# The recurrence of a two-layer decoder: the carried products' first half moved ahead of the values' products, and the sample's states summed over 80 rows

## The chip, the cores and the metric

The kernel runs on one core of one Trainium2 chip. The metric is the device time of one execution in microseconds (us), as the median of several executions. A core has engines that run side by side, each with its own instruction order: PE (matrix products, with PEld, the loading of its weights), DVE (vector), ACT (activations), POOL (GpSimd) and SP, which here mostly issues DMAs. PE works on 128 x 128 elements; a product can use all of it, 64 rows of it, or 64 columns of it, and two products that use different halves can run side by side. Results land in PSUM banks, and another engine has to copy them out before a bank is used again.

## The reference

One inference step of a decoder with two layers, a prompt of 1024 tokens behind 16 meta tokens, and a sample of 8 sequences with 8 tokens each. The first layer is an mLSTM, the second a forgetting attention; each is followed by a SwiGLU. The change lies in the mLSTM, whose recurrence goes over chunks of tokens. In a chunk, for each of 8 heads (`m_t` is a running maximum, `b` the summed log forget gates):

```python
s = jnp.einsum('bhtk,bhsk->bhts', q, k) * jnp.exp(dmat - m_t[..., None])
num = w_inter[..., None] * jnp.einsum('bhtk,bhkv->bhtv', q, C) + jnp.einsum('bhts,bhsv->bhtv', s, v)
den = w_inter * jnp.einsum('bhtk,bhk->bht', q, n) + jnp.sum(s, axis=-1)
h = num / jnp.maximum(jnp.abs(den), jnp.exp(-m_t))[..., None]
C_new = w_c[..., None, None] * C + jnp.einsum('bhs,bhsk,bhsv->bhkv', w_g, k, v)
```

In words: the scores `s` weigh the values of the chunk, the state `C` carried from earlier chunks is read with the queries, and the new state adds the chunk's keys and values. `n` runs along as a 129th column of `C`. The output `h` is normalised per head, multiplied with the sigmoid of an output gate and projected. The sample's tokens do the same, one chunk for each sequence, each with a state of its own.

## The kernel before

Everything is f32; a large product is split into three (high by high, high by low, low by high parts; `mm3`, lines 193 to 195). The tokens lie in nine tiles: tile 0 has 80 rows, 64 of the sample and 16 meta tokens, and tiles 1 to 8 have 128 prompt tokens each. A tile is a chunk of the recurrence.

`recurrence` (line 1155) writes the order of PE, DVE, ACT and POOL by hand: an instruction stands on its engine where the Python code issues it (`manual_schedule`). What it interleaves with the chunks is called fill: `f(1)` issues one step, three matmuls, of the output gates' product. Eight steps fill a PSUM bank (tag `mmA`, two banks); ACT then takes the sigmoid into `stg` (line 960) and POOL stores it to `ogD` (line 961). There are 192 such steps, and they run out within chunk 7. From then on `g` issues gate heads instead (`gate_head`, line 1549): three transposes on PE, the product with the gate on DVE (line 1559), a rounded copy on ACT (line 271) and the rest on DVE (line 272).

Iteration i of the loop does this for chunk i and the next ones, the code that issues it in brackets:

- scores of chunk i+1 (`chunk_scores`): eight 64-row products into two `sps` banks (line 1352), multiplied into `eb` on DVE (line 1354); two steps of fill; then its keys: four transposes into a bank `kps` of the same tag (line 1358), `kw` on DVE (line 1360), and the weighted queries `wb` (line 1362);
- the state (`chunk_state`): two banks `cp` of 64-column products (line 1391), added to `C` on DVE (line 1395), and on POOL `Cw`, the decayed state for the next chunk (line 1398);
- the decay of chunk i+2 (`decay_steps`): eight operations of DVE on `eb` (line 1335), whose exponential ACT takes later (line 1338);
- the output of chunk i (`chunk_out`): twice, for z = 0 and 1, values' products over the whole array (line 1453) and carried products of 64 rows (line 1457) into the two banks tagged `nps`; DVE copies the denominators (`den`, line 1415) and ACT the values (`vA`, line 1423), which frees the banks; at the end the exponential and the squares (line 1472);
- in iterations 3 and 6 the norm of the three chunks before (`norm_heads`, lines 1524 to 1542): five small DVE operations, a square root on ACT, two more and three long ones on DVE. The root needs another table in ACT than the sigmoid, and the exponential a third.

`chunk_load` (line 1268) has POOL issue the loads of `qk`, `eb` and `wb` of chunk i+2 at the head of iteration i, in POOL's queue with the stores to `ogD`.

Ahead of the loop, chunk 0 also updates the sample's eight states (`first_states`, line 1483): for four pairs of sequences and eight heads a product `cs` (line 1498) of the keys `km` (64 rows, masked by `bm` to one pair, line 1479) with the values, and on DVE the update of `C0` (line 1499), with a step of fill behind every second product. Behind the recurrence the output product (`pops`) starts, with weights `wo` that SP loads (line 512).

Of the kernel before, what the change touches and what calls it, by code (L numbers as in the profile page):

```python
# [8 lines left out]
F32 = mybir.dt.float32  # L9
# [8 lines left out]
P = 128  # L18
# [1015 lines left out]
def rec_prep(self, kp, gates, rp, pp):  # L1034
# [3 lines left out]
    if True:  # L1038
# [15 lines left out]
        for j in range(4):  # L1054
            for a in range(2):
# [14 lines left out]
                                channel_multiplier=1)  # L1070
        nc.gpsimd.affine_select(out=cap0[:, NS:], in_=cap0[:, NS:], compare_op=ALU.is_ge, fill=NEG, base=-NS,
                                pattern=[[0, NM]], channel_multiplier=1)
        bm = kp.tile([NS, NB], F32, name="bm")
        nc.gpsimd.memset(bm, 1.0)
        nc.gpsimd.affine_select(out=bm, in_=bm, compare_op=ALU.is_ge, fill=0.0, base=0, pattern=[[-8, 8]],
                                channel_multiplier=1)
# [77 lines left out]
@_add(Net)  # L1154
def recurrence(self, kp, rec, v, qkD, fill, gate):


    nc, I, O = self.nc, self.I, self.O
    eD, wD, cap, cap0, wcP, wcS, bm = rec
    tm, den, ssq = self.fin  # L1160

    self.fills = 0

    def f(n):
        for _ in range(n):
            next(fill, None)
            self.fills += 1

    C = self.C
    E = mybir.EngineType  # L1170
    with ExitStack() as cr, self.pool("recAp", bufs=2, space=PSUM) as pp:
        order = ExitStack()
        order.enter_context(self.tc.manual_schedule(engines={E.PE, E.DVE, E.Activation, E.Pool}))
        args = (pp, kp, C, v, qkD, eD, wD, tm)

        r0 = cr.enter_context(self.pool("rec0"))
        sets = {1: r0}
        load = lambda i: self.chunk_load(i, sets[i % 3], *args)
        with self.pool("sampA") as sp:
            R = self.chunk_load(0, r0, *args)  # L1180
            N = dict(eb=r0.tile([P, HA, P], F32, name="eb1", tag="eb", bufs=2))
            self.first_load(R, sp)
            f(4)
            self.chunk_decay(0, R, tm, cap0)
            R["exp"]()
            f(6)
            self.chunk_scores(0, R, r0, *args, f)
            self.first_queries(R, sp)
            f(2)
            self.first_sums(R, pp)  # L1190
            self.first_keys(0, R, bm)
            f(3)
            self.chunk_state(0, R, *args, wcP, f)
            N = self.chunk_load(1, r0, *args, **N)
            self.chunk_out(0, R, r0, *args, den, ssq, f, sp)

            ahead = r0.tile([P, HA, P], F32, name="eb2", tag="eb", bufs=2)
            nc.gpsimd.dma_start(ahead, eD[:, TT[2][0] : TT[2][1]].partition_broadcast(P))
            self.first_states(R, sp, pp, v, wcS, bm, f, self.decay_steps(1, N, tm, cap), N)
        with self.pool("rec2") as sets[2], self.pool("rec1", bufs=2) as rp, self.pool("rec3") as sets[0]:  # L1200
            R, N = N, self.chunk_load(2, sets[2], *args, eb=ahead, loaded=True)
            self.chunk_decay(2, N, tm, cap)
            N["exp"]()
            f(10)
            self.chunk_scores(1, R, rp, *args, f)
            g, norm = f, iter(())
            places = []
            gate = gate(places)
            for i in range(1, NT):
                N2 = load(i + 2) if i + 2 < NT else None  # L1210
                if i + 1 < NT:
                    f(12 if i == 1 else 3)
                    self.chunk_scores(i + 1, N, rp, *args, f)
                next(norm, None)
                g(2)
                self.chunk_state(i, R, *args, wcP, g)
                if i == NT - 1:
                    state = self.last_state(C[i % 2], pp, rp)
                    next(state)
                if N2:  # L1220
                    self.chunk_decay(i + 2, N2, tm, cap)
                next(norm, None)
                self.chunk_out(i, R, rp, *args, den, ssq, g, exp=N2 and N2["exp"],
                               then=(lambda: next(state, None)) if i == NT - 1 else None)
                for _ in norm:
# [64 lines left out]
@_add(Net)  # L1290
def first_load(self, R, sp):

    nc, I = self.nc, self.I

    W = 4 * 96 + 16
    qq = sp.tile([P, 512 + 2 * W], F32, name="qq")
    R["q2"] = qq[:, :512].rearrange("p (j z t) -> p j z t", z=2, t=NS)
    R["qms"] = [qq[:, 512 + z * W : 512 + z * W + W] for z in range(2)]
    R["y"] = [sp.tile([P, 2, DV], F32, name=f"y{g}") for g in range(4)]

    R["km"] = [sp.tile([NS, HA, 2, DK], F32, name="km0"),
               qq[:NS, : HA * P].rearrange("p (h a k) -> p h a k", h=HA, a=2)]
# [39 lines left out]
def chunk_scores(self, i, R, rp, pp, kp, C, v, qkD, eD, wD, tm, f):  # L1342
# [9 lines left out]
            nc.tensor.matmul(sps[g][:L, j, :L], qk[r, 4 + j, :L], qk[r, j, :L], start=True, stop=True)  # L1352
    for g in range(2):
        nc.vector.tensor_tensor(out=eb[:L, g::2, :L], in0=sps[g][:L, :, :L], in1=eb[:L, g::2, :L], op=ALU.mult)
    f(2 if i else 6)
    kps = pp.tile([P, 4, P], F32, name=f"kps{i}", tag="sps")
    for j in range(4):
        nc.tensor.transpose(kps[:L, j, :], qk[:, 4 + j, :L], self.ident)
# [41 lines left out]


@_add(Net)
def chunk_out(self, i, R, rp, pp, kp, C, v, qkD, eD, wD, tm, den, ssq, f, sp=None, exp=None, then=None):

    nc = self.nc
    L = TT[i][1] - TT[i][0]
# [16 lines left out]
            nc.scalar.copy(v(i)[:L, hx, :DV], ps[:L, :, :DV])  # L1423

    new = lambda g: pp.tile([P, 2, DV + 1], F32, name=f"nps{i}{g}", tag="nps")
    if i == 0:
        for g, hs in enumerate(((0, 2), (4, 6), (1, 3), (5, 7))):
            f(4)
# [13 lines left out]
            done(ps, g, hs)  # L1442
    else:

        for z in range(2):
            f(2 if z == 0 else 3)
            if z:
                f(3)
            ps = [new(2 * z + a) for a in range(2)]
            for a in range(2):  # L1450
                for x in range(2):
                    h = 4 * z + 2 * x + a
                    nc.tensor.matmul(ps[a][:L, x, :], at[:L, h, :L], v(i)[:L, h, :], start=(x == 0), stop=False)
            for x in range(2):
                for a in range(2):
                    r = slice(a * 64, a * 64 + 64)
                    nc.tensor.matmul(ps[a][:L, x, :], qw[r, 2 * z + x, :], Cp[r, 2 * z + x, :], start=False, stop=(x == 1))
            for a in range(2):
                done(ps[a], 2 * z + a, (4 * z + a, 4 * z + 2 + a))
        f(1)  # L1460
    if exp:
        exp()
    if then:
# [11 lines left out]
@_add(Net)  # L1475
def first_keys(self, j, R, bm):

    for a in range(2):
        self.nc.vector.tensor_scalar_mul(R["km"][j % 2][:, :, a, :], R["kw"][:NS], bm[:, 2 * j + a : 2 * j + a + 1])


@_add(Net)
def first_states(self, R, sp, pp, v, wcS, bm, f, steps, N):
# [3 lines left out]
    for j in range(4):  # L1487
        if j == 3:
            for _ in steps:
                pass  # L1490
            N["exp"]()
        else:
            self.first_keys(j + 1, R, bm)
        km = R["km"][j % 2]
        f(2)
        for h in range(HA):
            ps = pp.tile([P, DV + 1], F32, name=f"cs{j}{h}", tag="cps")
            nc.tensor.matmul(ps, km[:, h, :, :].rearrange("p a k -> p (a k)"), v(0)[:NS, h, :], start=True, stop=True)
            nc.vector.scalar_tensor_tensor(out=C0[:, j, h, :], in0=C0[:, j, h, :], scalar=wcS[:, j, h : h + 1],
                                           in1=ps, op0=ALU.mult, op1=ALU.add)  # L1500
            if h % 2:
                f(1)
                if j:
                    next(steps, None)
# [1541 lines left out]
```

## Time and profile before

| | us |
|---|---|
| runs of the kernel before | 2814.28, 2818.92, 2822.15 |
| their median | 2818.92 |
| the profiled execution, first to last instruction (span) | 2818.5 |
| PE busy, in the profiled execution | 2762.3 |
| DVE busy | 1798.8 |
| ACT busy | 1177.1 |
| POOL busy | 856.1 |

The profiled execution's time is its span and what lies around it; only the span is listed. It stands at the median of the runs. Times in rows of the profile are microseconds from the span's start. A row gives start, duration, engine, line, operation, output <- inputs, the tile of PE, the shape and a count of records; in square brackets stands the time for which the engine sat idle ahead of it and the instruction that ended the idle time. The recurrence takes the stretch from about 230 to 417 us. PE's clock was 0.994 of the full one in the mean of the span.

### The profile page before, as it was taken

The numbers are of one execution on the slowest core, as the hardware profiler recorded it, in microseconds if no ns is written. First come the engines' busy times: TensorE is split into PE (matmuls) and PEld (weight loads), VectorE is DVE, ScalarE is ACT, GpSimd is POOL, SyncE is SP. The second block draws the span as 40 slices with busy tenths as digits, with TensorE's granted clock in tenths as the row PEclk, the third lists the DMA queues.
The fourth block names the chain that finished last, engine by engine and source line by source line (L and its number), as shares of the span: only waits on it lengthen the run. The fifth ranks groups of instructions, "written<-read, shape, count | busy, mean of one in ns | idle before, by whom it ended". The sixth has DMA issues, their size and how long they took to land. (4 is left out here: it accounts for less than half of the span.)

```text
span 2818.5 us, 60631 instructions
## 1 busy us (share of the span) xinstructions
PE 2762.3 (98%) x23543; PEld 2650.7 (94%) x23543; DVE 1798.8 (64%) x4025; ACT 1177.1 (42%) x2299; POOL 856.1 (30%) x1348
## 2 busy tenths in 40 slices
PE   9999989999999999999999999999999999999998
PEld 8998879999999999999999887677999999999998
DVE  5633566888887655662455444776388888766656
ACT  5432553422223334443444455777343223323345
POOL 3142333223223232124452202444313223323111
PEclk9999999999999999999999999999999999999999
DMA  7666555355564375544443775432524655527556
GB/s 213 174 188 170 151 164 193 108 152 158 173 178 137 120 246 171 192 145 163 145 173 123 264 293 193 161 128 87 157 87 126 177 176 163 162 91 236 179 195 215
DMA packets 432420, 474.05 MB, mean 168 GB/s; under 512 B 37015, under 2 KB 358291, under 8 KB 431107
## 3 DMA queue, kind: packets, MB, share of 16 engines
q1 hardware_dynamic: 380562, 320.52, 36.9%
q0 software_dynamic: 44928, 143.44, 15.5%
q10 hardware_dynamic: 6640, 6.21, 0.7%
q8 instruction: 185, 3.03, 0.5%
q14 instruction: 105, 0.85, 0.1%
HBM read 322.84 MB, written 147.21 MB: 167 GB/s over the span
## 5 line engine op out<-in xcount | busy, mean ns | idle before, releaser
L1614 PE MATMUL m<-xh,slot 128*128 128x276 f32 x2752 | 541.0, 290 | 1.8 <-ACT fs L1643 1.8
L1614 PEld LDWEIGHTS m<-xh,slot 128*128 128x128 f32 x2752 | 440.1, 188 | 3.6 <-ACT fs L1643 2.2
L1614 PE MATMUL m<-xl,slot 128*128 128x276 f32 x1376 | 397.3, 289 | 0.0
L1614 PEld LDWEIGHTS m<-xl,slot 128*128 128x128 f32 x1376 | 259.0, 188 | 0.0
L193 PE MATMUL tmps<-slot,xh 128*128 128x256 f32 (+2 forms) x864 | 243.1, 281 | 0.0
L195 PE MATMUL tmps<-slot,xl 128*128 128x256 f32 (+2 forms) x864 | 240.6, 278 | 0.0
L194 PE MATMUL tmps<-slot,xh 128*128 128x256 f32 (+2 forms) x864 | 240.5, 278 | 0.0
L272 DVE TENSOR_TENSOR slot<-slot,slot 128x1024 fp32r<-128x1024 f32 x124 | 162.9, 1314 | 60.1 <-ACT slot L271 58.7
L271 ACT CAST slot<-slot 128x1024 fp32r<-128x1024 f32 x124 | 129.5, 1045 | 142.6 <-PE m L1614 111.7
L194 PEld LDWEIGHTS tmps<-slot,xh 128*128 128x128 f32 (+1 forms) x864 | 159.1, 184 | 0.1
L195 PEld LDWEIGHTS tmps<-slot,xl 128*128 128x128 f32 (+1 forms) x864 | 158.6, 184 | 0.0
L193 PEld LDWEIGHTS tmps<-slot,xh 128*128 128x128 f32 (+1 forms) x864 | 158.4, 183 | 0.2
L193 PE MATMUL mmA<-xh,whi 128*128 128x384 f32 (+1 forms) x384 | 135.2, 352 | 0.1
L195 PE MATMUL mmA<-xh,wlo 128*128 128x384 f32 (+1 forms) x384 | 128.2, 334 | 0.0
L194 PE MATMUL mmA<-xl,whi 128*128 128x384 f32 (+1 forms) x384 | 128.1, 334 | 0.0
L272 DVE TENSOR_TENSOR slot<-vA,slot 128x1024 fp32r<-128x1024 f32 (+1 forms) x59 | 82.2, 1396 | 32.7 <-ACT slot L271 31.5
L272 DVE TENSOR_TENSOR slot<-Ht,slot 128x1024 fp32r<-128x1024 f32 (+1 forms) x59 | 81.4, 1382 | 32.2 <-ACT slot L271 31.1
L271 ACT CAST slot<-Ht 128x1024 fp32r<-128x1024 f32 (+1 forms) x59 | 61.0, 1036 | 96.8 <-PE m L1614 92.9
L271 ACT CAST slot<-vA 128x1024 fp32r<-128x1024 f32 (+1 forms) x59 | 60.8, 1035 | 95.5 <-PE m L1614 88.5
L1718 DVE TENSOR_TENSOR ws<-ws 128x128 f32<-128x128 f32 x264 | 93.8, 355 | 8.9
L2868 ACT ACTIVATE s<-s,nb 128x272 f32<-128x272 f32 (+7 forms) x126 | 98.8, 786 | 0.0
L2903 ACT COPY th<-tp 128x768 f32<-128x768 f32 (+1 forms) x80 | 73.6, 920 | 55.9 <-PE tp L2895 32.8
(809 smaller groups left out, 8688.7 us busy)
## 6 DMA issues: line engine op xcount, KB each, us to landing
ws<-in_w_down SPq DMA_DIRECT2D x176, 128.0 KB, 2.7
sD<-ws SPq DMA_DIRECT2D x176, 128.0 KB, 2.1
slot<-sD SPq DMA_DIRECT2D x40, 512.0 KB, 4.0
slot<-in_w_gate_up SPq DMA_DIRECT2D x36, 512.0 KB, 4.1
kp<-in_cache_k SPq DMA_DIRECT2D x32, 512.0 KB, 7.1
vp<-in_cache_v SPq DMA_DIRECT2D x32, 512.0 KB, 5.5
vA<-in_w_gate_up SPq DMA_DIRECT2D x26, 512.0 KB, 3.9
Ht<-in_w_gate_up SPq DMA_DIRECT2D x26, 512.0 KB, 3.9
```

What stands on the lines that cost most here:

```text
L193: mm(ps, sh, mh, start=first, stop=False)
L194: mm(ps, sh, ml, start=False, stop=False)
L195: mm(ps, sl, mh, start=False, stop=last)
L271: self.nc.scalar.copy(hi, src)
L272: self.nc.vector.tensor_tensor(out=lo, in0=src, in1=hi.bitcast(F32), op=ALU.subtract)
L1614: nc.tensor.matmul(u.ps[h, b], w[p][:, k], x[q][:, k], start=first and k == i == 0, stop=k == 3 and i == 2, skip_group_check=True)
L1718: tt(out=o, in0=a, in1=b, op=ALU.subtract)
L2868: nc.scalar.activation(ss[z, u], ss[z, u], AF.Exp, bias=nb[:, z : z + 1], accum_out=sm[:, u, z : z + 1])
L2903: nc.scalar.copy(th.rearrange("p x z (u h q) -> p h (x z u) q", h=2, q=64)[:, :, :n], pt[:, :, :n])
```

## The change

It has two parts. The keys `km` and the mask `bm` of the sample's states get 80 partitions, not 64, and the product `cs` runs over 80 rows; the mask is 0 in the 16 rows of the meta tokens, so the sums are the same. And the loop's body is regrouped: the scores of the next chunk are followed at once by the carried products for z = 0 (which now open the bank, and the values' products close it) and by the state update; the keys of the next chunk (`chunk_keys`, cut out of `chunk_scores`), the decay and the norm come behind the output for z = 0; for z = 1 the order stays. A chunk's sixteen steps of fill stay sixteen: between its blocks stand 2, 7 and 7, where it was 2, 2, 2, 6 and 4.

```diff
-        bm = kp.tile([NS, NB], F32, name="bm")
+        bm = kp.tile([T0, NB], F32, name="bm")
...
             self.chunk_scores(1, R, rp, *args, f)
             g, norm = f, iter(())
-            places = []
+            places, state = [], None
             gate = gate(places)
             for i in range(1, NT):
                 N2 = load(i + 2) if i + 2 < NT else None
                 if i + 1 < NT:
                     f(12 if i == 1 else 3)
-                    self.chunk_scores(i + 1, N, rp, *args, f)
-                next(norm, None)
-                g(2)
-                self.chunk_state(i, R, *args, wcP, g)
-                if i == NT - 1:
-                    state = self.last_state(C[i % 2], pp, rp)
-                    next(state)
-                if N2:
-                    self.chunk_decay(i + 2, N2, tm, cap)
-                next(norm, None)
-                self.chunk_out(i, R, rp, *args, den, ssq, g, exp=N2 and N2["exp"],
-                               then=(lambda: next(state, None)) if i == NT - 1 else None)
+                    self.chunk_scores(i + 1, N, rp, *args, None)
+
+                def between():
+                    nonlocal state
+                    self.chunk_state(i, R, *args, wcP, g)
+                    if i == NT - 1:
+                        state = self.last_state(C[i % 2], pp, rp)
+                        next(state)
+                    if i + 1 < NT:
+                        f(2)
+
+                def after():
+                    if i + 1 < NT:
+                        self.chunk_keys(i + 1, N, pp, tm)
+                    if N2:
+                        self.chunk_decay(i + 2, N2, tm, cap)
+                    next(norm, None)
+                    g(2)
+                    g(3)
+                    g(2)
+                    next(norm, None)
+
+                self.chunk_out(i, R, rp, *args, den, ssq, g, exp=N2 and (lambda: N2["exp"]()),
+                               then=(lambda: next(state, None)) if i == NT - 1 else None, between=between, after=after)
                 for _ in norm:
                     pass
                 norm = self.norm_heads(i // 3, v, rp) if i % 3 == 2 else iter(())
...
+    if f is None:
+        return
     f(2 if i else 6)
+    self.chunk_keys(i, R, pp, tm)
+
+
+@_add(Net)
+def chunk_keys(self, i, R, pp, tm):
...
+    def carried(ps, first):
+        for x in range(2):
+            for a in range(2):
+                r, j = slice(a * 64, a * 64 + 64), x if first else 2 + x
+                nc.tensor.matmul(ps[a][:L, x, :], qw[r, j, :], Cp[r, j, :], start=(first and x == 0),
+                                 stop=(not first and x == 1), skip_group_check=True)
...
+        ps = None
         for z in range(2):
-            f(2 if z == 0 else 3)
-            if z:
-                f(3)
-            ps = [new(2 * z + a) for a in range(2)]
+            if z == 0:
+                ps = [new(a) for a in range(2)]
+                carried(ps, True)
+                between()
+            else:
+                ps = [new(2 + a) for a in range(2)]
             for a in range(2):
                 for x in range(2):
                     h = 4 * z + 2 * x + a
-                    nc.tensor.matmul(ps[a][:L, x, :], at[:L, h, :L], v(i)[:L, h, :], start=(x == 0), stop=False)
-            for x in range(2):
-                for a in range(2):
-                    r = slice(a * 64, a * 64 + 64)
-                    nc.tensor.matmul(ps[a][:L, x, :], qw[r, 2 * z + x, :], Cp[r, 2 * z + x, :], start=False, stop=(x == 1))
+                    nc.tensor.matmul(ps[a][:L, x, :], at[:L, h, :L], v(i)[:L, h, :], start=(z == 1 and x == 0),
+                                     stop=(z == 0 and x == 1), skip_group_check=True)
+            if z:
+                carried(ps, False)
             for a in range(2):
                 done(ps[a], 2 * z + a, (4 * z + a, 4 * z + 2 + a))
-        f(1)
+            if z == 0:
+                after()
+        f(2)
+        f(2)
...
-        self.nc.vector.tensor_scalar_mul(R["km"][j % 2][:, :, a, :], R["kw"][:NS], bm[:, 2 * j + a : 2 * j + a + 1])
+        self.nc.vector.tensor_scalar_mul(R["km"][j % 2][:, :, a, :], R["kw"][:T0], bm[:, 2 * j + a : 2 * j + a + 1])
...
-            nc.tensor.matmul(ps, km[:, h, :, :].rearrange("p a k -> p (a k)"), v(0)[:NS, h, :], start=True, stop=True)
+            nc.tensor.matmul(ps, km[:, h, :, :].rearrange("p a k -> p (a k)"), v(0)[:T0, h, :], start=True, stop=True)
```

PE's order in iteration 3 before, where the output for z = 0 begins (`mmA` is a bank of fill, L1453 the values' products, L1457 the first two of the four carried ones; the state product stands two steps of fill ahead of this, and the scores end eighteen rows ahead):

```order
L193 MATMUL mmA_4127<-xh,whi_3880 128x384
L194 MATMUL mmA_4127<-xl,whi_3880 128x384
L195 MATMUL mmA_4127<-xh,wlo_3881 128x384
L1453 MATMUL nps_4166<-vA,eb_3735 128x129 x2
L1453 MATMUL nps_4167<-vA,eb_3735 128x129 x2
L1457 MATMUL nps_4166<-C_105,wb_3737 128x129
L1457 MATMUL nps_4167<-C_105,wb_3737 128x129
```

and after the change, from the last two carried products on; the scores end two rows ahead, and the line numbers here and below are those of the changed kernel:

```order
L1454 MATMUL nps_4100<-C_105,wb_3737 128x129
L1454 MATMUL nps_4101<-C_105,wb_3737 128x129
L1414 MATMUL cp_4106<-vA,kw_3738 64x129 x4
L1414 MATMUL cp_4112<-vA,kw_3738 64x129 x4
L193 MATMUL mmA_4047<-xh,whi_3894 128x336
L194 MATMUL mmA_4047<-xl,whi_3894 128x336
L195 MATMUL mmA_4047<-xh,wlo_3895 128x336
```

The carried products have gone from behind the values' products to just behind the scores, and the state product (`cp`) follows them with no fill between.

DVE's order in the same iteration before, from behind `wb` on (`rd` and `fA` are the norm's, `den` the denominators of z = 0):

```order
L1531 SCALAR_TENSOR_TENSOR rd_4113<-den 128x24
L1532 TENSOR_TENSOR rd_4113<-rd_4113,tmA 128x24
L1533 RECIPROCAL rd_4113<-rd_4113 128x24
L1534 TENSOR_TENSOR fA_4114<-ssqA,rd_4113 128x24
L1535 TENSOR_TENSOR fA_4114<-fA_4114,rd_4113 128x24
L1395 TENSOR_TENSOR C_106<-C_107,cp_4136 128x258
L1395 TENSOR_TENSOR C_106<-C_107,cp_4142 128x258
L1335 SCALAR_TENSOR_TENSOR eb_4072<-eb_4072,tmA,cap 128x128 x8
L1538 RECIPROCAL fA_4114<-fA_4114 128x24
L1539 TENSOR_TENSOR fA_4114<-fA_4114,rd_4113 128x24
L1542 TENSOR_TENSOR vA<-vA,fA_4114 80x8x128
L1415 COPY den<-nps_4166 128x2
```

and after the change, from behind the two additions to `C` on:

```order
L1438 COPY den<-nps_4100 128x2
L1438 COPY den<-nps_4101 128x2
L1383 TENSOR_TENSOR kw_3924<-kps_4133,tmA 128x512
L1385 TENSOR_TENSOR wb_3923<-qk_3922,wb_3923 128x512
L1347 SCALAR_TENSOR_TENSOR eb_4072<-eb_4072,tmA,cap 128x128 x8
L1567 SCALAR_TENSOR_TENSOR rd_4148<-den 128x24
L1568 TENSOR_TENSOR rd_4148<-rd_4148,tmA 128x24
L1569 RECIPROCAL rd_4148<-rd_4148 128x24
L1570 TENSOR_TENSOR fA_4149<-ssqA,rd_4148 128x24
L1571 TENSOR_TENSOR fA_4149<-fA_4149,rd_4148 128x24
L1574 RECIPROCAL fA_4149<-fA_4149 128x24
L1575 TENSOR_TENSOR fA_4149<-fA_4149,rd_4148 128x24
```

The denominators have moved ahead of `kw` and the decay, and the norm's five small operations behind the decay.

ACT's order there before (`stg` evacuates a bank of fill, the first `vA` copies are those of z = 0):

```order
L1536 ACT_TABLE_LOAD
L1536 ACTIVATE fA_4114<-fA_4114,eps 128x24
L960 ACT_TABLE_LOAD
L960 ACTIVATE stg_4124<-mmA_4033 128x336
L259 CAST whi_4129<-wraw_4128 128x1024
L1423 COPY vA<-nps_4166 128x2x128
L1423 COPY vA<-nps_4167 128x2x128
L960 ACTIVATE stg_4196<-mmA_4127 128x384
L1423 COPY vA<-nps_4203 128x2x128
L1423 COPY vA<-nps_4204 128x2x128
```

and after the change:

```order
L1446 COPY vA<-nps_4100 128x2x128
L1446 COPY vA<-nps_4101 128x2x128
L1572 ACT_TABLE_LOAD
L1572 ACTIVATE fA_4149<-fA_4149,eps 128x24
L960 ACT_TABLE_LOAD
L960 ACTIVATE stg_4159<-mmA_4047 128x336
L259 CAST whi_4164<-wraw_4163 128x1024
L1446 COPY vA<-nps_4189 128x2x128
L1446 COPY vA<-nps_4190 128x2x128
L960 ACTIVATE stg_4210<-mmA_4162 128x384
```

The copies of z = 0 now stand ahead of the square root and its table, and the evacuation of the second bank behind the copies of z = 1.

On POOL the order is the same but for `Cw`, which now stands ahead of the first store to `ogD` of its iteration, and the loads of the next chunk but one, which stand behind the second store of the iteration before.

More of the change, by code (lines that the diff above doesn't have):

```diff
@@ L1299, in first_load @@
     R["y"] = [sp.tile([P, 2, DV], F32, name=f"y{g}") for g in range(4)]
-    R["km"] = [sp.tile([NS, HA, 2, DK], F32, name="km0"),
-               qq[:NS, : HA * P].rearrange("p (h a k) -> p h a k", h=HA, a=2)]
+    R["km"] = [sp.tile([T0, HA, 2, DK], F32, name="km0"),
+               qq[:T0, : HA * P].rearrange("p (h a k) -> p h a k", h=HA, a=2)]
     R["jk"] = sp.tile([P, DV], F32, name="jk0")
@@ L1354, in chunk_scores @@
         nc.vector.tensor_tensor(out=eb[:L, g::2, :L], in0=sps[g][:L, :, :L], in1=eb[:L, g::2, :L], op=ALU.mult)
+    if f is None:
+        return
     f(2 if i else 6)
+    self.chunk_keys(i, R, pp, tm)
+@_add(Net)
+def chunk_keys(self, i, R, pp, tm):
+    nc = self.nc
+    L = TT[i][1] - TT[i][0]
+    qk, qw = R["qk"], R["qw"]
     kps = pp.tile([P, 4, P], F32, name=f"kps{i}", tag="sps")
@@ L1402, in chunk_out @@
 @_add(Net)
-def chunk_out(self, i, R, rp, pp, kp, C, v, qkD, eD, wD, tm, den, ssq, f, sp=None, exp=None, then=None):
+def chunk_out(self, i, R, rp, pp, kp, C, v, qkD, eD, wD, tm, den, ssq, f, sp=None, exp=None, then=None, between=None, after=None):
     nc = self.nc
```

## The prediction

> **What bounds the kernel now.** I read the page first, then the engines' busy time in windows around the recurrence, then PE's timeline row by row there, and last what the other engines did in each of PE's waits.
>
> ```profile
> span 2818.5 us, 60631 instructions
> PE 2762.3 (98%) x23543; PEld 2650.7 (94%) x23543; DVE 1798.8 (64%) x4025; ACT 1177.1 (42%) x2299; POOL 856.1 (30%) x1348
> ```
>
> PE is the bound: 98% of the span. So only two things can move the time: PE time spent on the same products, and PE's waits. The changed stretch runs from about 265 us (sample's states) to the first output product at 416 us. Its windows (length, busy us of PE, PEld, DVE, ACT and POOL, granted clock, DMA share, GB/s):
>
> ```profile
> 229.00:265.00 36.00, 34.27 (x233) 32.57 (x232) 10.28 (x30) 10.02 (x26) 11.74 (x18) 0.91 0.56 140
> 380.00:393.00 13.00, 10.88 (x84) 9.84 (x84) 9.04 (x25) 5.99 (x11) 4.35 (x7) 1.00 0.31 85
> 393.00:417.00 24.00, 18.80 (x163) 15.32 (x162) 15.85 (x45) 13.51 (x45) 7.04 (x12) 0.93 0.53 176
> ```
>
> PE has holes in two of them: 2.1 us in chunk 6 (380 to 393) and 5.2 us in chunks 7 and 8 (393 to 417). The first window lies before the change and serves later as a price for the clock.
>
> **The cost of a block between two fills** (a fill is one matmul of the output gates here, a third of a step). One chunk on PE (columns: start, duration, engine, line, out<-in, tile, shape, records; an f32 matmul is two records, and two 64-row or 64-column matmuls run side by side):
>
> ```profile
> 303.49 0.34 PE L195 MATMUL mmA<-xh,wlo 128*128 128x384 f32 x1
> ...
> 305.13 0.34 PE L194 MATMUL mmA<-xl,whi 128*128 128x384 f32 x1
> ...
> 305.99 0.60 PE L1358 MATMUL kps<-ident,qk 128*128 128x128 f32 x4
> ...
> 306.61 0.34 PE L194 MATMUL mmA<-xl,whi 128*128 128x384 f32 x1
> ...
> 307.26 0.32 PE L195 MATMUL mmA<-xh,wlo 128*128 128x336 f32 x1
> 307.51 1.10 PE L1391 MATMUL cp<-vA,kw 128*64 128x129 f32 x16
> ...
> 308.80 0.32 PE L194 MATMUL mmA<-xl,whi 128*128 128x336 f32 x1
> ...
> 309.57 1.05 PE L1453 MATMUL nps<-vA,eb 128*128 128x129 f32 x8
> 310.55 0.72 PE L1457 MATMUL nps<-C,wb 64*128 64x129 f32 x8
> ...
> 311.46 0.32 PE L194 MATMUL mmA<-xl,whi 128*128 128x336 f32 x1
> ```
>
> From 305.13 to 305.99 stand five fills of 384 columns, 0.172 each; from 308.80 to 309.57 five of 336, 0.154 each. kps, on the full array, takes 306.61 - 305.99 = 0.62 with one fill: four records of 0.111 and no more. The scores (sps, tile 64*128, 16 records side by side) stand between the first two rows: 1.64 us. Two fills and eight steps of 0.111 would be 1.23, so the block costs **0.40 extra**. The state product (cp, 128*64): 1.54 against 2 x 0.154 + 8 x 0.111 = 1.20, **0.34 extra**. Values and carried products: 311.46 - 309.57 = 1.89 against 12 x 0.111 + 0.154 = 1.49, **0.40 extra**, put down to the 64-row carried ones, since the values' run in the full mode. So a block in another tile mode costs 0.34 to 0.40 us, about 0.19 for each of its two switches.
>
> The Trainium skill ("TensorEngine Tiling (Array Packing)", Key Properties) says that a change of the tiling mode, not of the tile, drains TensorE; the rows agree with a price for each such change. By that rule 64 rows to 64 columns is a change too.
>
> **Part 1, sample's states over 80 rows.** Two heads' product, then three fills, 16 times:
>
> ```profile
> 267.76 0.32 PE L195 MATMUL mmA<-xh,wlo 128*128 128x336 f32 x1
> 268.01 0.71 PE L1498 MATMUL cs<-vA,km 64*128 64x129 f32 x4
> ...
> 268.91 0.32 PE L194 MATMUL mmA<-xl,whi 128*128 128x336 f32 x1
> ...
> 257.26 0.39 PE L1432 MATMUL nps<-vA,eb 80*80 80x129 f32 x2
> ...
> 273.35 0.61 DVE L1499 SCALAR_TENSOR_TENSOR C<-C,wcS,cs 128x129 f32<-128x129 f32 x2 [0.43 <-PE cs L1498]
> ```
>
> A group takes 1.14 where two fills and four records would take 0.75: 0.39 extra. Over 80 rows it would run in the full mode; the 80-row product of chunk 0 (257.26) has two records in 0.39, one 0.11 behind the other, the pace of kps. 16 x 0.39 = 6.2. DVE, which follows the product, idles 0.43 us per group where a decay step stands beside it, so it can just keep up (0.04 left). Bounds 5.0 (DVE late in some groups) and 6.2; I take **6.0**.
>
> **Part 2, scores, carried products and state product in one block.** Before, a chunk had eight switches: two each for sps, cp and two carried halves. After, it has five: into rows, rows to columns, back to full, and two for the second carried half. Three times 0.19 is 0.57. No row of the recurrence shows rows to columns: free, the saving is 0.77; at a whole block's 0.40 it is 0.37. Nearest are the half prices above. Six chunks (1 to 6) x 0.58 = **3.5**, bounds 2.2 and 4.6.
>
> **Part 3, waits that go.** PE's waits on ACT's copies of an output bank (vA) and what made ACT late in chunk 6:
>
> ```profile
> PE nps L1453 <- ACT vA L1423: 3.3, 3, 2.1
> ...
> 389.38 1.16 PE L1453 MATMUL nps<-vA,eb 128*128 128x129 f32 x8 [2.12 <-ACT vA L1423]
> ...
> 412.87 2.09 PE L1453 MATMUL nps<-vA,eb 128*128 128x129 f32 x8 [0.97 <-ACT vA L1423]
> ...
> 383.74 3.42 DVE L1335 SCALAR_TENSOR_TENSOR eb<-eb,tmA,cap 128x128 f32<-128x128 f32 x8 [1.45 <-DMA eb<-eD]
> ...
> 388.77 0.22 DVE L1415 COPY den<-nps 128x2 f32<-128x2 f32 x2
> ...
> 388.95 0.65 ACT L1423 COPY vA<-nps 128x256 f32<-128x256 f32 x2 [5.22 <-DVE den L1415]
> ```
>
> In chunk 6 the den copies stood on DVE behind the decay, whose eb came late, and behind the norm; the copy waited 5.22 us for them, PE 2.12. The three waits make 3.3; less 2.12 and the tail's 0.97 the third, in chunk 3, is 0.2. The change puts the first half's den copies ahead of kw and decay, so both go: **2.4** (bounds 2.1 and 2.4).
>
> **Part 4, a wait that comes.** In chunks 3 and 6 ACT evacuates a finished fill bank behind the norm's square root:
>
> ```profile
> 381.99 1.28 ACT L960 ACT_TABLE_LOAD   x1
> 383.29 0.45 ACT L960 ACTIVATE stg<-mmA 128x336 f32<-128x336 f32 x1
> ...
> 335.29 0.69 DVE L1360 TENSOR_TENSOR kw<-kps,tmA 128x512 f32<-128x512 f32 x1 [0.16 <-PE kps L1358]
> ...
> 337.63 0.75 DVE L1395 TENSOR_TENSOR C<-C,cp 128x258 f32<-128x258 f32 x2
> 338.35 2.19 DVE L1335 SCALAR_TENSOR_TENSOR eb<-eb,tmA,cap 128x128 f32<-128x128 f32 x8
> ...
> eb<-eD POOLq DMA_DIRECT2D x4, 512.0 KB, 7.4
> ...
> eb<-eD POOLq DMA_DIRECT2D x1, 512.0 KB, 8.8
> ```
>
> Before, the root's inputs came right behind kw and wb; now the decay stands ahead of them. Count from the scores' start, T. PE: carried, cp, six fills, values, kps end at T + 5.1; the bank ends at 5.6 and is wanted again two banks on, at 11.5. DVE: kw from 5.3; kw, wb and the norm's five operations take 337.63 - 335.29 = 2.3, the decay 2.2; the root is done at 10.2. Then a table load of 1.28 and the evacuation of 0.45: 12.0, so PE waits 0.5 in each. If eb is late, all shifts. POOL issues eb's load behind the second bank's store, about 3.5 us after the second values' products, where the next T begins 21 fills (3.6 us) behind them; the load took 7.4 us in the median of chunks 3 to 6 and 8.8 in chunk 6 (the last two rows: KB, us from issue to landing). It lands near T + 7.3 and T + 8.7, against a decay due at 6.5: 0.8 and 2.2 late. PE's two waits are then 1.3 and 2.7, 4.0 in all, against 1.0 if eb is in time. I take **2.9**, nearer to the late end, since eb was late in chunk 6 before; bounds 0.5 and 4.5. In the other chunks no root stands there and the evacuation follows the copies at once, long before the bank is wanted, so there the moves cost nothing: the 21 fills behind the second products hide kw, decay and exponential.
>
> **Part 5, the tail.** Chunks 7 and 8 hold ten gate heads (gate_head: transposes on PE, then DVE, ACT, DVE):
>
> ```profile
> 393.41 0.38 PE L1352 MATMUL sps<-qk 64*128 64x128 f32 x2
> ...
> 401.39 0.55 DVE L1559 SCALAR_TENSOR_TENSOR ogeb<-ghps,gain,ogeb 128x336 f32<-128x336 f32 x1
> ...
> 402.91 0.56 DVE L1559 SCALAR_TENSOR_TENSOR ogeb<-ghps,gain,ogeb 128x336 f32<-128x336 f32 x1
> ...
> 409.34 0.55 POOL L961 DMA_DIRECT2D ogD<-stg  x1 [2.92 <-ACT stg L960]
> ...
> 416.52 0.37 PE L193 MATMUL pops<-xh,wo 128*128 128x276 f32 x1
> ...
> wo<-woD SPq DMA_DIRECT2D x6, 512.0 KB, 11.3
> ```
>
> The stretch is 23.1 us. A head occupies DVE and ACT for 1.52 (402.91 - 401.39), so ten need 15.2 whatever their order. Before, they began in chunk 7 behind kw; after, five still stand in chunk 7, but the last three fills and their evacuation fall between the fifth and sixth, and two heads behind the last products. Laid out with these durations the new order ends 0.5 later (23.6), with a PE hole near 3.5 us, hence some clock (0.5). The store at 409.34, 15.9 us in, frees buffers for the last wo loads; it moves about 2 us back, and the loads take 11.3. PE may then wait up to 4.3 for wo; I take 1.5, as 2 us are not all seen at pops. Together **2.5**, bounds -1 (switches saved, the wait of 0.97 gone) and 5.
>
> **Sum.** 6.0 + 3.5 + 2.4 - 2.9 - 2.5 = 6.5 us less, on the profile's 2818.5: 2812.0. The median of the runs is 2818.92, so **2812.4**.
>
> **The rivals.**
> - *No new waits*: eb lands sooner, since the queue is emptier, and the tail comes out even. Then 6.0 + 3.5 + 2.4 = 11.9 less: 2807.0. For it: the decay waited 1.45 only once in the rows above. Against it: the load is issued later than before.
> - *The grouping does not do what it says*: the array drains at each change of row group or of direction, and the block keeps its 1.2 us. Then part 2 is 0: 2815.9. Against it: sps itself alternates between two row groups without paying per pair.
> - *Slower, by the clock*: after a PE wait of 1.73 us (row below) the window 229 to 265 had a clock of 0.91, 36 x 0.09 = 3.2 us lost.
>
> ```profile
> 237.21 0.21 PE L1317 MATMUL n0p<-ident,n 32*128 32x32 f32 x1 [1.73 <-DMA n<-in_state_n]
> ```
>
> If chunk 6's new wait and both holes of the tail each cost that, 9.6 less the 1.7 that the tail loses now (24 x 0.07) are added to the forecast: 2820.3, slower than before. It decides once three such windows fall. Against it: the 2.12 us wait at 389.38 left the clock at 1.00. The Trainium skill ("TensorE: Matmul & The Clock Gate", What's actually happening) halves the clock after an idle window of about 3.4 us; by that only the tail's hole would count. The clock after the 1.73 us wait speaks against so long a window, the clock after the 2.12 us wait for it.
>
> **How the numbers follow.** Forecast 0.45, no new waits 0.33, grouping idle 0.14, clock 0.08. About 0.3% is what a measurement of this kernel can tell from no change: 8.5 us, so faster means below 2810.4 and slower above 2827.4. Faster: nearly all of the first rival (0.31) and the forecast's lower edge (0.09), 0.40. Slower: 0.03, if the clock rival meets the worst of the tail. Same: 0.57. The range reaches from 2804, the first rival with a gain of 3 in the tail and part 2, to 2820, the clock's.
>
> **What would show it.** Right: the cs groups' fills 0.75 apart, not 1.14, and tile 80*128; no switch gap between sps and carried; no wait on vA in chunk 6; a wait of the fills on ACT stg in chunks 3 and 6, with a table load ahead of it; a decay waiting for eb. Wrong: eb landing before T + 6.5; a clock under 0.9 in chunks 6 to 8; a wait for wo at pops over 4 us.

## The result and the profile after

| | median us | runs | ratio to before | 95% interval |
|---|---|---|---|---|
| before | 2817.45 | 17 | | |
| changed | 2812.67 | 17 | 0.9983 | 0.9976 to 0.9989 |

The change saves 4.8 us (0.17%; 3.1 to 6.8 us by the interval). The forecast was 2812.4 us and 6.5 us. The median of before has moved from 2818.92 to 2817.45 with more runs. The profiled execution of the changed kernel took 2814.68 us, and its span is 2813.1. With the same 1.6 us around its span, the profiled execution of before took about 2820.1 us, a little above its median and not at it. The first two lines of the new page answer to those shown of before:

```profile
span 2813.1 us, 60646 instructions
PE 2751.4 (98%) x23543; PEld 2648.8 (94%) x23543; DVE 1793.8 (64%) x4025; ACT 1176.6 (42%) x2299; POOL 855.1 (30%) x1348
```

PE is still the bound. Where the time went is read best from PE's waits between 225 and 440 us: us in total, times, the longest.

```profile
PE ghps L1594 <- DVE ogqk L1595: 3.3, 3, 1.7
PE mmA L193 <- ACT stg L960: 2.9, 2, 2.5
PE nps L1472 <- POOL C L1421: 2.4, 1, 2.4
PE n0p L1329 <- DMA n<-in_state_n: 1.6, 1, 1.6
PE pops L195 <- DMA wo<-woD: 1.5, 2, 1.3
PE ghps L1594 <- DVE ogeb L1595: 1.0, 2, 0.7
PE pops L193 <- DVE noP L1275: 1.0, 1, 1.0
```

No product waits for vA any more. The fills wait for ACT (2.9 us), and the output product for wo (1.5) and noP (1.0). The clock of the same windows as before (length, busy us of PE, PEld, DVE, ACT, POOL, granted clock, DMA share, GB/s):

```profile
229.00:265.00 36.00, 32.04 (x225) 30.42 (x225) 9.77 (x28) 9.68 (x25) 10.89 (x18) 0.95 0.60 144
...
380.00:393.00 13.00, 10.50 (x81) 9.62 (x80) 7.41 (x20) 8.42 (x26) 4.35 (x7) 0.87 0.25 84
393.00:417.00 24.00, 18.21 (x132) 14.94 (x131) 16.02 (x52) 12.26 (x36) 7.23 (x13) 0.86 0.53 167
```

In chunk 6 (380 to 393) the clock is 0.87, where it was 1.00, and in chunks 7 and 8 (393 to 417) it is 0.86, where it was 0.93.

Laid side by side, PE's timelines of the two kernels give the gain as it builds up (start of the same instruction, us):

| PE begins | before | changed | difference |
|---|---|---|---|
| first cs (sample's states) | 265.35 | 266.73 | +1.4 |
| nnp, behind the sample's states | 289.78 | 285.53 | -4.2 |
| scores in iteration 1 | 303.75 | 299.50 | -4.2 |
| scores in iteration 2 | 318.04 | 313.21 | -4.8 |
| scores in iteration 3 | 332.53 | 327.10 | -5.4 |
| scores in iteration 4 | 347.63 | 341.73 | -5.9 |
| scores in iteration 5 | 361.93 | 355.45 | -6.5 |
| scores in iteration 6 | 376.42 | 369.32 | -7.1 |
| scores in iteration 7 | 393.41 | 387.72 | -5.7 |
| first output product | 416.52 | 411.24 | -5.3 |
| its sixth group of eight products (`pops`) | 433.42 | 431.46 | -2.0 |

The first row is not the change's: in chunk 0, which it leaves as it was, PE waits 2.4 us ahead of a product with the sample's old states (L1472) in the new profile; the old one has no wait there, but a lower clock over the same window (0.91 beside 0.95). All the later profiles, with either order and with 64 or 80 rows, have this wait (2.3 to 2.7 us), so here the one profile of before stands apart. Behind the last row the two profiles drift apart and together by several us (from -2.0 to +0.6 and to -5.4 at the end) in parts that the change doesn't touch. So the stages are compared by their traces and the whole by the medians.

### The profile page after: what moved, and what is told of

It is laid out like the page before. It is cut to its first block, busy times and chain, and to the rows that moved or that the text cites. A ratio compares the mean times of both kernels' runs of the same rounds, so it can differ in the third digit from the quotient of the medians.

```text
span 2813.1 us, 60646 instructions
## 1 busy us (share of the span) xinstructions
PE 2751.4 (98%) x23543; PEld 2648.8 (94%) x23543; DVE 1793.8 (64%) x4025; ACT 1176.6 (42%) x2299; POOL 855.1 (30%) x1348
```

## The experiments

The theory after the result: the states save 5.6 us; grouping saves 0.6 a chunk; the waits that come cost 2.9 us in the fills, a lower clock behind the longer one, and some 3 us at the output product. Each is undone or done alone below. The runs of before are shared by the kernels of a batch: 2816.52 us in the median of 27 runs for the first four, 2816.77 of 21 for the others.

| | median us | runs | ratio to before | 95% interval |
|---|---|---|---|---|
| states over 80 rows alone | 2812.84 | 11 | 0.9984 | 0.9975 to 0.9993 |
| regrouping alone | 2817.85 | 12 | 1.0005 | 0.9997 to 1.0014 |
| changed, root ahead of the decay | 2808.55 | 7 | 0.9972 | 0.9961 to 0.9983 |
| changed, loads early | 2808.61 | 7 | 0.9966 | 0.9955 to 0.9977 |
| changed, fill between scores and carried | 2817.94 | 1 | | |
| changed, last step of fill in chunk 7 | 2811.49 | 11 | 0.9980 | 0.9971 to 0.9989 |
| the same and noP early | 2809.07 | 11 | 0.9974 | 0.9965 to 0.9983 |
| all four edits | 2805.22 | 5 | 0.9962 | 0.9949 to 0.9976 |

**The states alone.** The kernel before with the four lines of the sample's states:

```diff
-        bm = kp.tile([NS, NB], F32, name="bm")
+        bm = kp.tile([T0, NB], F32, name="bm")
...
-            nc.tensor.matmul(ps, km[:, h, :, :].rearrange("p a k -> p (a k)"), v(0)[:NS, h, :], start=True, stop=True)
+            nc.tensor.matmul(ps, km[:, h, :, :].rearrange("p a k -> p (a k)"), v(0)[:T0, h, :], start=True, stop=True)
```

> The kernel before with the 80-row sample's states alone. Theory (the switch of tile mode is paid per group, and nothing later eats the gain): a cs group with its three fills goes from 1.30 us to about 0.97, the stretch from the first cs to nnp shrinks by 5.6 us (5.0 to 6.2), no new wait of the fills or cs on DVE, and the time falls by about the same, to 2811.8 beside 2817.4. Rival (the states end earlier but the loads of the next chunks and wo do not, so PE waits for them): the stretch shrinks alike, but new waits between it and the output product eat most of it, 2816 to 2817.

Its PE timeline, one group of the states:

```profile
266.58 0.67 PE L1498 MATMUL cs<-vA,km 80*128 80x129 f32 x4
267.00 0.40 PE L193 MATMUL mmA<-xh,whi 128*128 128x336 f32 x1
267.24 0.32 PE L194 MATMUL mmA<-xl,whi 128*128 128x336 f32 x1
267.40 0.32 PE L195 MATMUL mmA<-xh,wlo 128*128 128x336 f32 x1
267.56 0.62 PE L1498 MATMUL cs<-vA,km 80*128 80x129 f32 x4
```

The tile is 80*128, and a group takes 0.98 us (267.56 - 266.58), where it was 1.30. From the first cs to nnp it is 5.7 us less than before, and the scores of iterations 1 to 6 all start 6.3 us earlier: up to there nothing eats it. Iteration 7 and the first output product start 5.1 us earlier, since the clock in chunk 6 was 0.87 in this profile (the last section shows it); no wait for wo came. The time falls by 0.16%, 4.5 us (2.0 to 7.0). The theory holds, the rival falls. This kernel also has the wait of chunk 0 (2.6 us), with the order of before there, so that wait has nothing to do with the regrouping.

**The regrouping alone.** The changed kernel with the same lines turned back to NS.

> The changed kernel with the 64-row sample's states put back, that is the regrouped loop alone. Theory (grouping saves 0.6 us in each of seven chunks, two waits of 2.4 us go, but the fills' wait of 2.9 us on ACT, a slower clock after it, about 1.7 us, and waits of about 3.3 us at the output product come): net between 1 us faster and 2 us slower than before, 2816.5 to 2819.5, with the same waits as in the changed kernel at the same places. Rival (the waits come only because the chunks start 4 to 6 us earlier against loads that do not): the waits shrink and the regrouping alone brings 3 us or more, 2814 or less.

```profile
PE mmA L193 <- ACT stg L960: 4.0, 2, 3.0
PE ghps L1594 <- DVE ogqk L1595: 3.8, 3, 1.7
PE nps L1472 <- POOL C L1421: 2.7, 1, 2.7
PE pops L195 <- DMA wo<-woD: 2.1, 2, 1.2
...
PE pops L193 <- DVE noP L1275: 1.0, 1, 1.0
```

The same waits stand at the same places though the chunks start later, so they come from the new order and not from the earlier start. The ratio is 1.0005 (0.9997 to 1.0014): by itself the regrouping is worth between 0.8 us less and 3.9 us more, that is nothing that can be told.

**The root ahead of the decay.**

```diff
                     if i + 1 < NT:
                         self.chunk_keys(i + 1, N, pp, tm)
+                    next(norm, None)
                     if N2:
                         self.chunk_decay(i + 2, N2, tm, cap)
-                    next(norm, None)
```

> The changed kernel with the first half of the norm (five DVE operations and the square root) put ahead of the decay instead of behind it. Theory (the fills wait for a bank whose evacuation stands on ACT behind a root whose inputs stand on DVE behind a decay that waits for eb): the waits of the fills on ACT, 0.4 and 2.5 us in chunks 3 and 6, go to 0, the clock in chunk 6 goes from 0.87 back to 1.00, and 4 to 4.6 us are saved up to chunk 7; time about 2808 to 2810 beside 2812.7. Rival (late eb is the cause by itself): the decay still waits 2 us, the wait moves to the copies of the second half or to the next scores, and at most 0.5 us is saved.

DVE in chunk 6 there:

```profile
374.80 0.18 DVE L1567 SCALAR_TENSOR_TENSOR rd<-den 128x24 f32<-128x24 f32 x1
...
375.86 0.18 DVE L1571 TENSOR_TENSOR fA<-fA,rd 128x24 f32<-128x24 f32 x1
377.42 2.19 DVE L1347 SCALAR_TENSOR_TENSOR eb<-eb,tmA,cap 128x128 f32<-128x128 f32 x8 [1.38 <-DMA eb<-eD]
```

The decay still waits for eb, 1.38 us, but the root's inputs are done ahead of it and nothing of PE waits behind it: between 290 and 382 us PE has no wait left, and the clock of 380 to 393 is 1.00. From iteration 1's scores to iteration 7's the chunks gain 6.4 us on before, where the changed kernel gained 1.4. At iteration 7 that is 4.9 us ahead of the changed kernel. The time falls to 2808.55 us; by the ratios 3 us less than the changed kernel, with intervals that overlap, so the time alone doesn't show it. The theory holds by the trace; in this order a late eb by itself costs nothing.

**The loads early.** The loads of chunk i + 3 are issued right behind the second products of chunk i, whose buffers they take:

```diff
             if z == 0:
                 after()
+        soon()
         f(2)
         f(2)
```

where `soon` keeps `load(i + 3)` for the iteration after.

> The changed kernel with the loads of qk, eb and wb issued on POOL right behind the second products of the chunk whose buffers they take, ahead of the store of the next bank. Theory (eb is late because its issue stands behind that store): eb is issued about 2 us earlier relative to the scores, the decay's wait of 2.1 us in chunk 6 falls below 0.5, the fills' wait there from 2.5 to about 0.5, the clock stays at 1.00; 3 to 4 us saved, about 2809. Rival (the load takes longer because wo loads share the DMA engines then, it lands at the same time): the decay waits as before and nothing is saved.

POOL and DVE around chunk 6:

```profile
365.41 0.90 POOL L1297 DMA_DIRECT2D eb<-eD  x1 [1.06 <-PE nps L1491]
366.29 1.25 POOL L1302 DMA_DIRECT2D wb<-wD  x2
367.70 0.57 POOL L961 DMA_DIRECT2D ogD<-stg  x1 [0.16 <-issue]
```

```profile
374.85 0.68 DVE L1389 TENSOR_TENSOR wb<-qk,wb 128x512 f32<-128x512 f32 x1
375.45 2.19 DVE L1351 SCALAR_TENSOR_TENSOR eb<-eb,tmA,cap 128x128 f32<-128x128 f32 x8
```

eb is issued 3.7 us ahead of the scores (at 369.12), where the changed kernel issued it 0.2 us behind them, the decay runs on without a wait, and the fills' two waits sum to 0.7 us, 0.4 in chunk 3 and 0.3 in chunk 6. Clock in 380 to 393: 1.00. At iteration 7 this kernel is 3.8 us ahead of the changed one, and its median is 2808.61 us, by the ratios 5 us less, with intervals that barely overlap. The rival falls: the load took 6.6 us there, where the changed kernel's took 8.3. Both edits cure the same wait, one at the root and one at eb.

**A step of fill between scores and carried products**, and one less behind the state product:

```diff
                 ps = [new(a) for a in range(2)]
+                if i + 1 < NT:
+                    fill(1)
                 carried(ps, True)
                 between()
```

> The changed kernel with one step of fill (three matmuls) moved from behind the state product to between the scores and the carried products, so that the 64-row block is cut in two. Theory (a price of about 0.19 us for each switch of tile mode): each of chunks 1 to 6 is 0.38 to 0.40 us longer than in the changed kernel, read from the start of one chunk's scores to the next, about 2.4 us over six. Rival (the regrouping gained by something else, such as the order of values and carried products): the chunks keep their length.

The block of iteration 2 there, with the step of fill inside it:

```profile
312.35 1.16 PE L1364 MATMUL sps<-qk 64*128 64x128 f32 x16
313.44 0.44 PE L193 MATMUL mmA<-xh,whi 128*128 128x384 f32 x1
...
314.15 0.72 PE L1454 MATMUL nps<-C,wb 64*128 64x129 f32 x8
```

Read from one iteration's scores to the next: iteration 1 takes 14.11 us against 13.71 in the changed kernel, iteration 2 14.32 against 13.89, iteration 4 14.09 against 13.72, iteration 5 14.33 against 13.87. That is 0.37 to 0.46 more each, the price of the two switches (the iterations with a root differ by their waits as well). The rival falls. This rests on the trace of a single execution; its time is not compared.

**The last step of fill in chunk 7.**

```diff
                     if i + 1 < NT:
-                        f(2)
+                        f(3 if i == NT - 2 else 2)
```

> The changed kernel with the very last step of fill issued in chunk 7, one step earlier in the same run of fill, instead of between two gate heads in chunk 8. Theory (the last bank's store lands late, and the last loads of wo wait for it; the sigmoid's table load stands between gate heads): the last wo loads are issued some 8 us earlier, PE's wait of 1.5 us for wo goes, the heads' wait of 0.5 us on the evacuation goes; about 3 us saved up to the sixth output group, 2809 to 2811. Rival (the wo loads wait for something else, the gate heads' buffers or the freed pools): they are issued as late as before and less than 1 us is saved.

SP's issues, in this kernel (first row) and in the changed one (second and third):

```profile
388.89 8.16 SPq L512 DMA_DIRECT2D wo<-woD  x6
```

```profile
405.87 10.28 SPq L512 DMA_DIRECT2D wo<-woD  x6
...
414.37 1.78 SPq L512 DMA_DIRECT2D wo<-woD  x4
```

The last four wo loads of the changed kernel were issued from 414.37 on; here all six are out by 397, at least 17 us earlier (8 were expected; this execution was already 3 us ahead at iteration 7's scores), and the wait for wo is gone. That they waited for the last bank's store is shown. From iteration 7's scores to the first output product it takes 21.3 us, not 23.5. The heads' wait of 0.5 us on the evacuation went too, and a wait of 1.0 us for vA came at the head of chunk 8 (396.75). But a new wait stands behind the first output product:

```profile
PE pops L195 <- DMA slot<-woD: 1.4, 2, 1.0
```

The output product now waits for its next weights, in other buffers. So some of the gain is given back, 2811.49 us against 2812.67, just outside the 2809 to 2811 that were expected; the two intervals overlap, and the time alone doesn't tell them apart.

**noP early besides.**

```diff
                     if i + 1 < NT:
                         self.chunk_keys(i + 1, N, pp, tm)
+                    else:
+                        next(state, None)
```

> As the kernel with the last step of fill in chunk 7, and besides the transposition and copy of the last normaliser state (nnpP, noP) are issued right behind the first output half of chunk 8 instead of at its end. Theory (the second output group takes the bank that noP still has to empty): the wait of 1.0 us of the output product on noP goes, so 0.8 to 1.0 us less than without this. Rival (the bank is not what it waits for, but the weights or the last gate head): the wait stays, put down to another.

The wait on noP is gone, and another stands at the new place of the transposition, which must wait for a copy (nnP) that stands on DVE behind the squares and the state (the row names the copy of den that starts 0.1 us behind nnP's):

```profile
406.83 0.27 PE L1275 MATMUL nnpP<-ident,nnP 128*4 128x128 f32 x1 [1.79 <-DVE den L1440]
```

Inconclusive by the time: 2809.07, 2.4 us under the kernel without it by the medians, where 0.8 to 1.0 were expected, with intervals that overlap (0.9965 to 0.9983 and 0.9971 to 0.9989); the trace shows one wait traded for another. That the bank was what the output product waited for is shown, since the wait went with the earlier copy and no wait came in its place there.

**All four.**

> The changed kernel with all four edits: root ahead of the decay, early loads, last step of fill in chunk 7, early noP. Theory (the first two cure the same waits, 4 to 5 us, the last two the tail's, 3 to 4 us): 7 to 9 us less than the changed kernel, 2804 to 2806, 0.4 to 0.5% below the kernel before. Rival (behind the recurrence the product is bound by the loads of its weights, which come no earlier): the recurrence ends 7 to 9 us earlier, but the output product gives back half, 2808 or more.

2805.22 us, 0.9962 of before (0.9949 to 0.9976), the best median of all; by the ratios 6 us under the changed kernel, where 7 to 9 were expected, with intervals that touch. The first output product starts at 403.45, 7.8 us ahead of the changed profile, 1.0 of it from ahead of the first chunk. At the eighth group of the output product 7.3 us are left, so the net loss there is small, not half as the rival had it. But two things lie in that net. Without the waits for noP and wo the lead had grown to 11.2 us at the sixth group (420.28 beside 431.46), and a new wait, with the slower clock behind it, took 3.9 of it:

```profile
PE ghps L1601 <- DVE ogc L1602: 2.1, 1, 2.1
```

```profile
424.95 0.62 DVE L1602 SCALAR_TENSOR_TENSOR ogc<-ghps,gain,ogc 128x384 f32<-128x384 f32 x1 [3.41 <-DMA ogc<-ogD]
```

A gate head among the output products waits on DVE for the load of its gates (`ogc`), PE waits 2.1 us for that head, and the clock from 423 to 432 was 0.81. So a load does bind there, as the rival had it, though it is the gates' and not the weights'.

## Why the prediction was right

The time lay 0.3 us from the forecast; the gain was 4.8 us where 6.5 was said. The closeness of the time is luck: the median of before moved down by 1.5 us with more runs, and from 2817.45 the same sum gives 2811.0, 1.7 us too low. The mechanisms of the sum were there, with two costs that it had too small. The gain lies under the 0.3% that the prediction took as the least that can be told; with seventeen runs of each kernel its interval is clear of no change. Term by term:

- **Part 1, states, 6.0:** 5.6 us in the changed kernel (from +1.4 to -4.2), 5.7 alone. Right; the 6.2 of the arithmetic weren't all there, as allowed for.
- **Part 2, grouping, 3.5:** 0.6 in each iteration without a root. The block itself shows the unknown price of rows to columns:

```profile
312.94 0.34 PE L195 MATMUL mmA<-xh,wlo 128*128 128x384 f32 x1
313.21 1.16 PE L1364 MATMUL sps<-qk 64*128 64x128 f32 x16
314.21 0.61 PE L1454 MATMUL nps<-C,wb 64*128 64x129 f32 x8
314.75 1.10 PE L1414 MATMUL cp<-vA,kw 128*64 128x129 f32 x16
...
316.06 0.34 PE L194 MATMUL mmA<-xl,whi 128*128 128x384 f32 x1
```

  From 312.94 to 316.06 it is 3.12 us; two fills of 0.172 and twenty steps of 0.111 make 2.56. The 0.56 extra are three switches at 0.19 each, as taken. Right.
- **Part 3, waits that go, 2.4:** both are gone. Right.
- **Part 4, the fills' wait, 2.9:** measured 2.9, in its parts 0.4 and 2.5 where 1.3 and 2.7 were said. The exact hit is luck: in the four other profiles that leave the root and the loads as in the changed kernel (the regrouping alone, the fill between, the last step, the last step and noP early) the two waits sum to 3.1 to 4.0 us, still within the bounds. The chain in chunk 6 is the forecast one:

```profile
377.85 2.19 DVE L1347 SCALAR_TENSOR_TENSOR eb<-eb,tmA,cap 128x128 f32<-128x128 f32 x8 [2.11 <-DMA eb<-eD]
...
381.23 0.31 ACT L1572 ACTIVATE fA<-fA,eps 128x24 f32<-128x24 f32 x1 [5.35 <-DVE fA L1571]
381.56 1.28 ACT L960 ACT_TABLE_LOAD   x1
382.86 0.45 ACT L960 ACTIVATE stg<-mmA 128x336 f32<-128x336 f32 x1
...
383.36 0.49 PE L193 MATMUL mmA<-xh,whi 128*128 128x384 f32 x1 [2.50 <-ACT stg L960]
```

  The decay starts 8.5 us behind the scores (377.85 - 369.32; 8.7 was said). In chunk 3 it starts at 6.3 without a wait: there eb came in time, and the 0.4 left are the 0.5 of the layout without a late eb. In the four other profiles eb came 0.4 to 0.7 us late there, and the wait was 0.8 to 1.1. The undoing of either link takes the long wait away: to nothing by the root's place, to 0.3 us by eb's issue.
- **The clock in chunk 6** was not in the sum; it was a rival's. Behind the 2.50 us wait the fills run at 0.32 instead of 0.17 apart for 3.5 us, and the window's clock of 0.87 makes 13 x 0.13 = 1.7 us. This is the step that failed: the forecast's sum let chunk 6's new wait cost only its length. The rival had 3.2 for it, twice what it was. The prediction's own list of signs of being wrong holds a clock under 0.9 in chunks 6 to 8, and that sign came, 0.87 and 0.86; the price was smaller than the rival's, so the time stayed near the forecast.
- **Part 5, tail, 2.5:** up to the first output product 0.4 longer (0.5 was said, and 0.5 for the clock), the wait for wo 1.5 as taken. The hole near 3.5 us did not come, the longest wait before the output product is 1.7; the clock fell all the same. What it missed is the wait of 1.0 us for noP: the second output group takes the PSUM bank of nnpP, and noP's copy stands on DVE behind the last gate head (noP at 415.20, the product at 415.53):

```profile
415.20 0.27 DVE L1275 COPY noP<-nnpP 4x128 f32<-4x128 f32 x1
```

```profile
415.53 0.40 PE L193 MATMUL pops<-xh,wo 128*128 128x276 f32 x1 [1.00 <-DVE noP L1275]
```

  The three waits make 2.5 us; with the slower restart behind each (some 0.3 us) the output product gives back 3.3 us, from -5.3 to -2.0, twice the 1.5 of the sum.

So the two terms missing are 1.7 us of clock and about 1.8 us at the output product; 6.5 less these is 3.0, beside 3.4 in the traces (-2.0 less chunk 0's +1.4) and 3.1 to 6.8 by the medians. The median lies 1.4 above what the traces show up to there; that part stays open, since it lies in stretches that the change doesn't touch. The rival "no new waits" falls, as does "the grouping does not do what it says". The split by parts is clear now: the sample's states bring all of the gain, and the regrouping pays for its own 6 us with its new waits and the lower clock behind them.

## What to carry to other kernels

Here grouping products by tile mode paid what the counted switches said (0.6 us an iteration, 0.58 forecast), so it could be priced from one block of the trace; but a regrouping moves whole queues on the engines behind it, and a new wait on PE can cost more than its length. Look for each instruction that now stands behind a DMA's wait on its engine (here the decay ahead of the root's inputs) and ask whose buffer waits for what is queued there. A wait that was new on PE was cured as well by moving the five small operations in front of the late one as by loading earlier.

## What the runs showed of the hardware

The clock behind a PE wait in chunk 6 does not follow the length of the wait alone. Over the same window, 380 to 393 us, the profiles show for the longest wait in chunk 6 and the granted clock (the regrouping alone waits later, so its window is 388 to 401):

| kernel | wait us | clock |
|---|---|---|
| root ahead of the decay | none | 1.00 |
| all four edits | none | 1.00 |
| loads early | 0.3 | 1.00 |
| states alone | 1.9 | 0.87 |
| last step of fill in chunk 7 | 2.1 | 1.00 |
| before | 2.1 | 1.00 |
| changed | 2.5 | 0.87 |
| fill between scores and carried | 2.8 | 0.74 |
| last step and noP early | 2.8 | 0.74 |
| regrouping alone | 3.0 | 0.87 |

Rows of one of them:

```profile
382.77 1.16 PE L1453 MATMUL nps<-vA,eb 128*128 128x129 f32 x8 [1.85 <-ACT vA L1423]
383.86 1.23 PE L1457 MATMUL nps<-C,wb 64*128 64x129 f32 x8
385.02 0.69 PE L193 MATMUL mmA<-xh,whi 128*128 128x384 f32 x1
385.50 0.52 PE L194 MATMUL mmA<-xl,whi 128*128 128x384 f32 x1
385.82 0.52 PE L195 MATMUL mmA<-xh,wlo 128*128 128x384 f32 x1
```

These rows are of the kernel with the states alone: a wait of 1.85 us, and the fills take 0.32 each behind it (385.82 - 385.50). The kernel before had 2.12 us at the same instruction and full clock. So a wait of about 2 us on PE may cost its length alone or 1.7 us more; 2.8 us cost 3.4 more (13 x 0.26) in both profiles that had it, and 3.0 us again 1.7 more. At 0.3 us nothing was lost. Each clock here is the mean of a window in one execution. The Trainium skill ("TensorE: Matmul & The Clock Gate", What's actually happening) says that the clock is set by a free-running window of about 3.4 us. By an estimate from that figure, one such window at half the clock loses 1.7 us and two lose 3.4, which agrees with the runs, as does the unequal lot of the waits near 2 us with a window that doesn't start with the wait. That page of the Trainium skill asks for an idle window before the clock falls; the runs show it fall behind waits of 1.9 us, well below one.
